# A list schedule with slack before readers on other engines, and with transfers planned at 320 GB/s for 180

## The chip, the cores and the metric

The kernel runs on one core of one Trainium2 chip. The metric is device time in microseconds (us) of one execution; less is better. The core has five engines that work through their own instruction queues in order and wait for each other by semaphores: TensorE (PE, matmuls and transposes; its weight loads are shown as PEld), VectorE (DVE), ScalarE (ACT), GpSimd (POOL) and SyncE (SP, which here issues all transfers). PE writes to PSUM, ACT and DVE read its results there.

## The reference

It is a decoder trunk of two layers on a sequence of 1024 rows of width 1024, in float32.

```python
# layer A: differential attention, 8 heads, each with two pairs (q1,k1), (q2,k2) of width 64
h = rms(x, a_norm)
q, k, v, g = split(h @ a_w_in)                     # 1024 columns each
q, k = rope_partial(rms(q)), rope_partial(rms(k))  # per head and half
a = softmax(mask(q1 @ k1.T / 8)) - lam * softmax(mask(q2 @ k2.T / 8))
o = rms(a @ v, subln) * (1 - lambda_init)
x = x + (o * silu(g)) @ a_w_out
# shared keys and values, then layer B: stick-breaking attention, 16 heads of width 64
k, v = split(rms(x, kv_norm) @ w_kv)
q, g = split(rms(x, b_norm) @ b_w_in)
z = q @ k.T / 8
log_1mb = where(mask, log_sigmoid(-z), 0)
suffix = cumsum_from_the_right(log_1mb) - log_1mb
a = where(mask, exp(log_sigmoid(z) + suffix), 0)
out = x + ((a @ v) * silu(g)) @ b_w_out
```

## The kernel before, in words

Every float32 product is made of three reduced-precision ones: both operands are split into a high and a low part (ACT copies the high part, DVE subtracts), and PE multiplies high by high, high by low and low by high. So a step of a projection is a triple of matmuls into one `proj` accumulator, of 256 or 512 columns. Weights come from DRAM as 256 KB loads into one of three `raw` buffers and are split into `w` tiles (`split_w`); layer A also splits the weights of layer B in advance and writes them back to DRAM (`park`: a `raw` load, a split with `ph` as the high part, two stores).

The work is a sequence of heads. For a head, `qkv_a` or `qkv_b` makes q, k and v by projection; in layer A, q and k are normalised and rotated in a tile `qk` (ACT, DVE, then four instructions on POOL) and transposed by PE (`tr<-ident,qk`). `unit_s` computes scores (`sc`, 64-row matmuls) of blocks of 128 rows and works them into a row of weights `zl` (A: minimum, exponential, sum, normalisation; B: exponential, logarithm, a scan on DVE called `u4k`, exponential). `unit_t` transposes these rows (`tr<-ident,zl`), splits them into `th` and `tl`, and multiplies by the values (`av`). Gated outputs go to DRAM (`og_a`, `og_b`) and come back for the out-projection (`OutProj`), which adds them to residual rows `xr`; those rows are loaded into buffers that held keys and values (`kh`, `kl`, `v`) in `open_rows`. PSUM has two `proj`, three `tr`, one `av` and one double `sc` buffer.

`run_layer` interleaves two threads in the recording: the attention of one head, and as filler the projections of the next head (for the last head: the out-projection of the first half of the rows). What is recorded is not yet the order. Every call goes into `Order.add`, which notes its engine, what it depends on, its priority (its place in the recording, shifted by `rec.priority`) and two planned costs from `Order.cost`: how long it holds its engine, and the lag until others see its result. `Order.issue` is a list scheduler: it goes through planned time, lets each free engine take the ready instruction with the best priority whose buffer is free, and writes the order in which they were taken. Each engine's queue is then that order. An instruction's end, in the plan, releases its readers on other engines and its buffers; readers on the same engine are released when the engine is free. For transfers the plan has one queue: a transfer starts 1.2 us after its issue or behind the one before, takes its size over a rate, and lands 0.8 us later. The plan decides the order alone; on the chip the semaphores decide when.

All compute instructions are emitted by one line of `issue`, so all rows of the profile carry that line, L374; the change moves it to L377.

Of the kernel before, what the change touches and what calls it, by code (L numbers as in the profile page):

```python
# [32 lines left out]
def f32(ap):  # L33
    return ap.bitcast(F32)

class Root:
# [111 lines left out]
class Order:  # L150
# [86 lines left out]
    def cost(self, eng, method, a, kw):  # L237
        n = int(np.prod(a[0].idx.shape)) if isinstance(a[0], L) and a[0].root.space != "dram" else 1
        src = a[1] if len(a) > 1 else None
        if eng == "pe":  # L240
            mv = a[2] if method == "matmul" else a[1]
            if method == "transpose" or mv.dt == F32:
                return n * 0.109 / 128 * (1 if n <= 128 else 2 if n < 512 else 2), 0.17
            t = {512: 0.228, 384: 0.172, 256: 0.12}[n]
            return (t / 2, 0.17) if a[1].p[1] - a[1].p[0] == 64 else (t, 0.17)
        psum = isinstance(src, L) and src.root.space == "psum"
        if eng == "act":
            by = isinstance(kw.get("scale"), L)
            return (0.18 if by else 0.08) + (0.00078 if psum else 0.00086) * n + (0.19 if "accum_out" in kw else 0), 0.17
        if eng == "dve":  # L250
            if method == "tensor_tensor_scan":
                return 0.06 + 0.0021 * n, 0.15
            if method in ("tensor_scalar", "tensor_copy", "memset") and not psum:
                return 0.12 + 0.00055 * n, 0.15
            if method in ("tensor_reduce", "reduce_sum"):
                n = int(np.prod(src.idx.shape))
            if method == "scalar_tensor_tensor":
                return 0.12 + 0.00103 * n, 0.15
            return 0.065 + 0.00105 * n + (0.05 if method == "tensor_tensor_reduce" else 0), 0.15
        if eng == "pool":  # L260
            if method == "affine_select":
                return 0.74 + 0.0008 * n, 0.06
            return (0.13 + 0.0006 * n if method == "memset" else 0.1 + 0.0028 * n), 0.06
        k = a[0] if isinstance(a[0], L) and a[0].root.space != "dram" else a[1]
        size = (k.p[1] - k.p[0]) * int(np.prod(k.idx.shape)) * 4
        return 0.07, size / 180e3

    def issue(self, prepare):

# [9 lines left out]
        early = sum(map(in_la, self.ops))  # L279
        live, nxt = dict.fromkeys(queue, 0), dict.fromkeys(queue, 0)  # L280
        placed, blocked = set(), {s: [] for s in [*queue, None]}
        ready, free = {e: [] for e in self.ENGINES}, dict.fromkeys(self.ENGINES, 0.0)
# [32 lines left out]
        while len(order) < len(self.ops) or events:  # L315
            issued = False
            for e in self.ENGINES:
                if free[e] > now:
                    continue
                while ready[e]:  # L320
                    _, no = heapq.heappop(ready[e])
                    op = self.ops[no]
                    slot = missing(op)
                    if slot != ():
                        blocked[slot].append(no)
                        continue
                    for r in sorted(op.roots, key=lambda r: r.no):
                        if r.slot and r not in placed:
                            placed.add(r)
                            live[r.slot] += 1  # L330
                            nxt[r.slot] += 1
                            unblock(r.slot)
                    op.at, free[e] = now, now + op.took
                    if e == "sp":
                        dma = max(now + 1.2, dma) + op.lag
                        end = dma + 0.8
                    else:
                        end = free[e] + op.lag
                    order.append(op)
                    heapq.heappush(events, (free[e], 0, no))  # L340
                    heapq.heappush(events, (end, 1, no))
                    issued = True
                    break
            if issued:
                continue
            assert events, "no order"
            now = events[0][0]
            while events and events[0][0] <= now:
                _, ended, no = heapq.heappop(events)
                op = self.ops[no]  # L350
                let(op, not ended)
                if not ended:
                    continue
                if in_la(op):
                    early -= 1
                    if not early:
                        unblock(None)
                for r in op.roots:
                    r.left -= 1
                    if r.slot and not r.left:  # L360
                        live[r.slot] -= 1
                        unblock(r.slot)
        self.span = now
        real = lambda x: x.real() if isinstance(x, L) else x
        with self.tc.manual_schedule():
            for op in order:
# [5 lines left out]
                e = self.real[op.eng]  # L372
# [4 lines left out]
def build(tc, ins, out):  # L377
# [7 lines left out]

    mk = lambda name, bufs, **kw: ctx.enter_context(tc.tile_pool(name=name, bufs=bufs, **kw))
    B = {"proj": 2, "sc": 2, "tr": 3, "av": 1, "th": 3, "g2k": 3, "o": 6, "w": 8, "raw": 3, "ta": 1, "g1k": 2, "hpr": 1, "small": 9, "qk": 2, "hpe": -1, "hpw": -1,
         "al": 6, "bl": 8, "tb": 3, "oa": 0, "la": 0, "lb": 8, "lt": 0, "lead": 1.0, "leada": 0.02, "leadb": 0.02, "leadxa": 0.15, "leadxb": 0.1, "holda": 0, "holdb": 0, "c2": 1, "gca": 0, "gcb": 0, "prea": 2, "preb": 1, "warm": 16, "wp": 2, "hpx": -1, "nx": 1, "nk": 6, "hpo": 0, "ob": 2, "late": 400, "ph": 2}
    ORDERS = ((0, 1, 2, 3), (3, 0, 2, 1), (1, 3, 0, 2), (2, 0, 3, 1), (3, 2, 1, 0), (1, 2, 0, 3), (0, 2, 1, 3), (2, 3, 0, 1),
              (1, 0, 3, 2), (3, 2, 0, 1), (2, 3, 1, 0), (1, 0, 2, 3))  # L390
    cp = mk("const", 1)
# [359 lines left out]
    def gate_mul(hd, h, og):  # L751
        for hf in range(2):
            assert hd.done[hf] == 2 and hd.sg[hf] is not None
            o, hi = hd.o[hf], hd.sg[hf].bitcast(F32R)
            pool.tensor_tensor(o, o, hd.sg[hf], ALU.mult)
            (act.copy if B["gc" + "ab"[layer[1]]] else dve.tensor_copy)(hi, o)
            pool.tensor_tensor(o.bitcast(F32R), o, f32(hi), ALU.subtract)
            sp.dma_start(og[hf, 0, :, h, :], f32(hi))
            sp.dma_start(og[hf, 1, :, h, :], o)
# [93 lines left out]
    def run_layer(hds, qkv, unit_s, unit_t, xT, og, op, hfs, extra=()):  # L853
# [5 lines left out]
        f1 = 1 - f0  # L859
# [60 lines left out]
        for h in range(n - 1):  # L920
            main = []
            for i, m in enumerate(order):
                main += unit_s(h, m)
                main += late
                if i == 0 and h > 0:
# [7 lines left out]
        ma, mb, mc, md = last_order  # L933
        op.open_rows(f0, True)
        ss = unit_s(h, ma)
        main = (late + ss if B["lt"] else ss + late) + [(0.0, lambda: gate_mul(hds[h - 1], h - 1, og)),
                                       (0.0, lambda: op.open(f0, op.nk0, n - 1))]
        main += unit_s(h, mb) + unit_t(h, ma) + unit_t(h, mb)
        merge(main, steps[hold:] + fill(n), B["lead"])
        op.finish_gate(f0)  # L940
        main = unit_s(h, mc) + [(0.0, lambda: op.open(f1, 0, n - 1))] + unit_s(h, md) + unit_t(h, mc) + unit_t(h, md)
        steps = fill(n + 1) + [(0.0, lambda: op.open_rows(f1, False))] + fill(n + 2)
        merge(main, steps, B["lead"])
        op.finish_gate(f1)
# [372 lines left out]
```

## Time and profile before

| | |
|---|---|
| median of 3 runs | 1488.15 us (1487.16 to 1489.11) |
| profiled execution | 1487.93 us, span 1486.1 us |
| PE busy | 1403.6 us (94%) |
| weight loads busy | 1181.0 us (79%) |
| DVE, ACT, POOL busy | 1080.6, 920.8, 299.3 us |
| granted TensorE clock, mean | 0.981 |
| moved by transfers | 185.93 MB, 125 GB/s on average |

Layer A ends and layer B starts at about 640 to 720 us; from 1421 us on only the last out-projection is left. In the views by stretches a row has the stretch, its length, the busy time and the number of instructions of PE, PEld, DVE, ACT and POOL in it, the granted clock of TensorE (1 is 2.4 GHz, and half of it the lower level), the busy share of the transfer engines and GB/s. A row of waits has the engine that stood with what it was to write, the engine and tile that released it, the total time, how often, and the longest. In a timeline, what stands in brackets is the idle time of the engine just before the instruction and what ended it.

### The profile page before, as it was taken

To read this page: it belongs to the slowest core of one execution; us is meant where nothing else is said; L and a number is where in the kernel's file an instruction comes from. 1 tells how busy PE (TensorE), PEld (TensorE's weight loads), DVE (VectorE), ACT (ScalarE), POOL (GpSimd) and SP (SyncE) were. 2 spreads that over 40 slices of the span, in tenths; PEclk is the share of its full clock that TensorE was granted. 3 is DMA by queue.
4 is the path that set the end of the run, shared out by engine and by line. 5 is a ranking of instruction groups with operands and counts; after the bars stand their busy time and mean duration, and the time that the engine had idled before them with its cause. 6 is when DMAs were issued, how large, how long until landed. Compare 5 with 4: busy or idle time off the path is not lost.

```text
span 1486.1 us, 24678 instructions
## 1 busy us (share of the span) xinstructions
PE 1403.6 (94%) x8944; PEld 1181.0 (79%) x8944; DVE 1080.6 (73%) x2145; ACT 920.8 (62%) x1834; POOL 299.3 (20%) x545
## 2 busy tenths in 40 slices
PE   7999999999999999868999999999999999998999
PEld 6887878787878787757988777777777878787899
DVE  6588787888888888764531869687878786979941
ACT  6576666666666665432332868686868686878610
POOL 0112221121222121100000124142423241424100
PEclk8999999999999999978999999999999999999999
DMA  5045544454554456343252212121212121143724
GB/s 199 29 150 164 167 153 158 138 175 148 164 177 161 148 182 208 133 179 126 79 170 97 74 58 86 58 86 57 85 54 75 55 74 58 64 168 138 284 85 143
DMA packets 94603, 185.93 MB, mean 125 GB/s; under 512 B 8721, under 2 KB 43793, under 8 KB 93457
## 3 DMA queue, kind: packets, MB, share of 16 engines
q1 hardware_dynamic: 94480, 184.35, 36.9%
q8 instruction: 71, 1.16, 0.3%
q14 instruction: 52, 0.42, 0.1%
HBM read 119.31 MB, written 65.01 MB: 124 GB/s over the span
## 4 chain that ended last, share of the span: by engine, by line
PE 29%; DVE 19%; ACT 9%; issue 3%; POOL 0%; DMA 0%; SPq 0%; DVEq 0%; ACTq 0%; POOLq 0%
PE proj L374 20%; DVE u4k L374 12%; PE av L374 4%; ACT u4k L374 3%; ACT zl L374 3%; PE tr L374 3%; DVE tl L374 2%; PE sc L374 2%; DVE zl L374 1%; DVE o L374 1%; ACT o L374 1%; DVE kl L374 1%; DVE v L374 1%; DVE g2k L374 1%; DVE small L374 0%
## 5 line engine op out<-in xcount | busy, mean ns | idle before, releaser
L374 PE MATMUL proj<-ah,w 128*128 128x512 f32 x1536 | 542.6, 403 | 0.0
L374 PE MATMUL proj<-w,ah 128*128 128x256 f32 x1984 | 382.0, 292 | 7.1 <-ACT w L374 2.7
L374 PEld LDWEIGHTS proj<-ah,w 128*128 128x128 f32 x1536 | 289.0, 188 | 69.6 <-issue 15.4
L374 PEld LDWEIGHTS proj<-w,ah 128*128 128x128 f32 x1984 | 313.9, 194 | 19.3 <-issue 5.8
L374 PE MATMUL proj<-al,w 128*128 128x512 f32 x768 | 300.2, 391 | 0.0
L374 PE MATMUL proj<-w,al 128*128 128x256 f32 x992 | 283.1, 285 | 0.2 <-DVE al L374 0.2
L374 PEld LDWEIGHTS proj<-w,al 128*128 128x128 f32 x992 | 192.3, 194 | 0.7 <-DVE al L374 0.7
L374 DVE TENSOR_TENSOR_SCAN u4k<-zl,u4k 128x768 f32<-128x768 f32 (+4 forms) x96 | 176.7, 1841 | 3.0
L374 PE MATMUL tr<-ident,zl 128*128 128x128 f32 x992 | 152.1, 284 | 22.7 <-DVE zl L374 19.4
L374 ACT ACTIVATE th<-tr 128x512 fp32r<-128x512 f32 (+1 forms) x240 | 126.4, 551 | 67.5 <-PE tr L374 64.5
L374 DVE TENSOR_TENSOR tl<-tr,th 128x512 fp32r<-128x512 f32 (+1 forms) x240 | 144.1, 628 | 32.7 <-ACT th L374 32.0
L374 PE MATMUL av<-th,v 128*128 128x256 f32 x640 | 155.0, 294 | 10.1 <-DVE o L374 5.9
L374 ACT ACTIVATE u4k<-u4k 128x768 f32<-128x768 f32 (+4 forms) x192 | 159.0, 843 | 7.3 <-DVE u4k L374 4.6
L374 PEld LDWEIGHTS proj<-al,w 128*128 128x128 f32 x768 | 144.9, 189 | 19.9
L374 PE MATMUL sc<-kh,q 64*128 64x512 f32 (+2 forms) x768 | 141.8, 387 | 16.4 <-DVE small L374 9.6
L374 PEld LDWEIGHTS tr<-ident,zl 128*128 128x128 f32 x992 | 119.7, 145 | 45.2 <-issue 21.3
L374 PE MATMUL av<-tl,v 128*128 128x256 f32 x480 | 135.4, 302 | 6.4 <-DVE tl L374 5.4
L374 PEld LDWEIGHTS av<-th,v 128*128 128x128 f32 x640 | 113.3, 193 | 29.6 <-issue 11.6
L374 POOL TENSOR_TENSOR o<-o,o 128x512 f32<-128x512 f32 (+1 forms) x56 | 87.9, 1570 | 186.1 <-DVE o L374 171.4
L374 ACT ACTIVATE zl<-zl,small 128x256 f32<-128x256 f32 (+7 forms) x128 | 98.2, 769 | 43.3 <-DVE small L374 43.3
L374 PEld LDWEIGHTS sc<-kh,q 64*128 64x128 f32 x768 | 70.3, 186 | 61.8 <-issue 19.1
L374 DVE SCALAR_TENSOR_TENSOR u4k<-zl,u4k 128x768 f32<-128x768 f32 (+4 forms) x96 | 94.1, 981 | 31.8 <-ACT u4k L374 31.2
(120 smaller groups left out, 1922.3 us busy)
## 6 DMA issues: line engine op xcount, KB each, us to landing
w<-w_kv SPq DMA_DIRECT2D x32, 512.0 KB, 5.1
w<-w_b SPq DMA_DIRECT2D x32, 512.0 KB, 5.0
w<-w_o SPq DMA_DIRECT2D x24, 512.0 KB, 5.7
raw<-in_w_kv_dram SPq DMA_DIRECT2D x32, 256.0 KB, 2.8
w_kv<-ph SPq DMA_DIRECT2D x32, 256.0 KB, 2.2
w_kv<-raw SPq DMA_DIRECT2D x32, 256.0 KB, 2.4
raw<-in_w_b_dram SPq DMA_DIRECT2D x32, 256.0 KB, 2.8
w_b<-ph SPq DMA_DIRECT2D x32, 256.0 KB, 2.5
```

The source lines that it names most:

```text
L374: getattr(e, method)(*[real(x) for x in a], **{k: real(v) for k, v in kw.items()})
```

## The change

Three numbers of the planner are changed; the recorded program is the same. On the planned end of every compute instruction, as others see it, 0.4 us are added. The planned rate of transfers is 320 GB/s instead of 180. In the last head of each layer the attention's steps are recorded with a priority shifted by `-B["ahead"]`, which is 0.

```diff
+MARGIN = 0.4
...
     def cost(self, eng, method, a, kw):
...
-        return 0.07, size / 180e3
+        return 0.07, size / 320e3
...
     def issue(self, prepare):
...
                         dma = max(now + 1.2, dma) + op.lag
                         end = dma + 0.8
                     else:
-                        end = free[e] + op.lag
+                        end = free[e] + op.lag + MARGIN
                     order.append(op)
                     heapq.heappush(events, (free[e], 0, no))
                     heapq.heappush(events, (end, 1, no))
...
+        ahead = lambda steps: [(c, lambda st=st: early(st)) for c, st in steps]
+
+        def early(st):
+            with rec.priority(-B["ahead"]):
+                st()
+
-        main = (late + ss if B["lt"] else ss + late) + [(0.0, lambda: gate_mul(hds[h - 1], h - 1, og)),
+        main = ahead(ss) + late + [(0.0, lambda: gate_mul(hds[h - 1], h - 1, og)),
                                        (0.0, lambda: op.open(f0, op.nk0, n - 1))]
-        main += unit_s(h, mb) + unit_t(h, ma) + unit_t(h, mb)
+        main += ahead(unit_s(h, mb) + unit_t(h, ma) + unit_t(h, mb))
...
-        main = unit_s(h, mc) + [(0.0, lambda: op.open(f1, 0, n - 1))] + unit_s(h, md) + unit_t(h, mc) + unit_t(h, md)
+        main = ahead(unit_s(h, mc)) + [(0.0, lambda: op.open(f1, 0, n - 1))] + ahead(unit_s(h, md) + unit_t(h, mc) + unit_t(h, md))
```

The first place is on PE at the passage from layer A to layer B, before the change. Names are tile, number in the recording and a running number: `sc_1691` are the last scores of layer A's last head, `tr_1707` transposes of the rows `zl_1677` and `zl_1687` made from its last two score steps.

```order
L374 MATMUL tr_1707_8248<-ident_70,zl_1677_8171 128x128
L374 MATMUL tr_1710_8250<-ident_70,zl_1677_8171 128x128
L374 MATMUL tr_1713_8252<-ident_70,zl_1677_8171 128x128
L374 MATMUL sc_1691_8259<-kh_1431_7191,q0_1489_7414 128x512 x2
L374 MATMUL sc_1691_8259<-kl_1432_7198,q0_1489_7414 128x512 x2
L374 MATMUL sc_1691_8259<-kh_1431_7191,q1_1490_7429 128x512 x2
L374 MATMUL tr_1707_8248<-ident_70,zl_1687_8254 128x128
L374 MATMUL tr_1707_8248<-ident_70,zl_1677_8171 128x128
```

The same place in the changed order, where `proj_1763` and `proj_1775` are groups of the out-projection; the dots stand for 3 and for 63 rows, all of the out-projection.

```order
L377 MATMUL sc_1691_8573<-kh_1431_7216,q0_1489_7458 128x512 x2
L377 MATMUL sc_1691_8573<-kl_1432_7229,q0_1489_7458 128x512 x2
L377 MATMUL sc_1691_8573<-kh_1431_7216,q1_1490_7478 128x512 x2
L377 MATMUL proj_1763_8536<-w_1727_8276,ah_1547_7519 128x256
L377 MATMUL proj_1763_8536<-w_1728_8290,ah_1547_7519 128x256
L377 MATMUL proj_1763_8536<-w_1727_8276,al_1548_7521 128x256
...
L377 MATMUL proj_1775_8591<-w_1628_8039,ah_1672_8044 128x256
L377 MATMUL proj_1775_8591<-w_1629_8056,ah_1672_8044 128x256
L377 MATMUL proj_1775_8591<-w_1628_8039,al_1673_8066 128x256
...
L377 MATMUL tr_1707_8552<-ident_70,zl_1687_8557 128x128
L377 MATMUL tr_1707_8552<-ident_70,zl_1677_8433 128x128
```

Before, the transposes of `zl_1687` follow the scores at once; now 72 projection matmuls, single rows all, stand between them.

The second place is SP at the passage, before the change: `raw<-in_a_w_out` loads weights of the out-projection, `kh_1773` and `kl_1774` are residual rows in buffers of keys, `w2_o` stores parked weights.

```order
L374 DMA kh_1773_8267<-in_x_dram 128x1024
L374 DMA kl_1774_8269<-in_x_dram 128x1024
L374 DMA w2_o_87<-ph_1537_8293 128x512
L374 DMA raw_1550_8308<-in_b_w_out_dram 128x512
L374 DMA w2_o_87<-raw_1536_8085 128x512
L374 DMA raw_1632_8345<-in_a_w_out_dram 128x512
L374 DMA w2_o_87<-ph_1551_8357 128x512
L374 DMA w2_o_87<-raw_1550_8308 128x512
L374 DMA raw_1633_8362<-in_a_w_out_dram 128x512
L374 DMA raw_1634_8372<-in_a_w_out_dram 128x512
L374 DMA raw_1635_8384<-in_a_w_out_dram 128x512
```

And in the changed order, from the same load of `raw_1550` on; the dots stand for 15 rows, 10 of them loads of `raw<-in_a_w_out`.

```order
L377 DMA raw_1550_7896<-in_b_w_out_dram 128x512
L377 DMA raw_1632_7910<-in_a_w_out_dram 128x512
L377 DMA w2_o_87<-raw_1536_7775 128x512
L377 DMA w2_o_87<-ph_1551_7952 128x512
L377 DMA raw_1633_7975<-in_a_w_out_dram 128x512
...
L377 DMA raw_1793_8328<-in_a_w_out_dram 128x512
L377 DMA x1_80<-kh_1562_7583 128x1024
L377 DMA x1_80<-kl_1563_7586 128x1024
L377 DMA x1_80<-qk_1564_7214 128x1024
L377 DMA kh_1773_8587<-in_x_dram 128x1024
L377 DMA kl_1774_8589<-in_x_dram 128x1024
```

The loads of `raw_1632` to `raw_1793` stood behind that of `kh_1773` and stand ahead of it now.

The third place is PE in layer A before the change: the transposes of `qk_967` (those at 401.42 us in the trace) with the score step ahead of them.

```order
L374 MATMUL sc_1024_5100<-kh_797_4169,q0_804_4158 128x512 x2
L374 MATMUL sc_1024_5100<-kl_798_4190,q0_804_4158 128x512 x2
L374 MATMUL sc_1024_5100<-kh_797_4169,q1_805_4177 128x512 x2
L374 MATMUL proj_1031_5071<-w_873_4420,ah_4_371 128x256
L374 MATMUL proj_1031_5071<-w_874_4432,ah_4_371 128x256
L374 MATMUL proj_1031_5071<-w_873_4420,al_5_380 128x256
L374 MATMUL tr_1005_5119<-ident_70,qk_967_4815 128x128 x4
L374 MATMUL tr_1008_5127<-ident_70,qk_967_4815 128x128 x4
```

And now, where `proj_1041` is the next group of rows after `proj_1031`; the dots stand for 6 rows of the two projection groups.

```order
L377 MATMUL sc_1024_5125<-kh_797_4214,q0_804_4203 128x512 x2
L377 MATMUL sc_1024_5125<-kl_798_4229,q0_804_4203 128x512 x2
L377 MATMUL sc_1024_5125<-kh_797_4214,q1_805_4219 128x512 x2
L377 MATMUL proj_1031_5086<-w_873_4327,ah_4_364 128x256
L377 MATMUL proj_1031_5086<-w_874_4338,ah_4_364 128x256
L377 MATMUL proj_1031_5086<-w_873_4327,al_5_380 128x256
...
L377 MATMUL proj_1041_5149<-w_871_4286,ah_4_364 128x256
L377 MATMUL proj_1041_5149<-w_872_4304,ah_4_364 128x256
L377 MATMUL proj_1041_5149<-w_871_4286,al_5_380 128x256
L377 MATMUL tr_1005_5160<-ident_70,qk_967_4807 128x128 x4
L377 MATMUL tr_1008_5172<-ident_70,qk_967_4807 128x128 x4
```

From the last matmul of `proj_995`, which completes `qk_967`, to these transposes the old order has 39 projection matmuls and two score steps, the new one 54 and the same two steps.

## Rows read from the trace of the kernel before

**Rows 1.** The page: busy time of each engine, and PE in 40 equal slices.
```profile
PE 1403.6 (94%) x8944; PEld 1181.0 (79%) x8944; DVE 1080.6 (73%) x2145; ACT 920.8 (62%) x1834; POOL 299.3 (20%) x545
...
PE   7999999999999999868999999999999999998999
```

**Rows 2.** Busy time of layer A and of layer B between their ends.
```profile
100.00:600.00 500.00, 475.78 (x3188) 403.36 (x3185) 409.26 (x1038) 326.10 (x745) 102.22 (x144) 1.00 0.52 167
720.00:1300.00 580.00, 568.33 (x3270) 455.07 (x3268) 414.17 (x553) 394.28 (x679) 147.79 (x294) 1.00 0.23 76
```

**Rows 3.** Busy time around the passage from layer A to layer B.
```profile
640.00:650.00 10.00, 5.79 (x30) 4.39 (x31) 7.04 (x20) 3.61 (x7) 0.00 (x0) 0.66 0.93 354
650.00:660.00 10.00, 5.18 (x28) 3.02 (x27) 5.97 (x20) 4.47 (x9) 0.00 (x0) 0.80 0.15 51
660.00:670.00 10.00, 6.27 (x31) 6.27 (x32) 5.32 (x9) 3.89 (x9) 0.41 (x2) 0.52 0.43 152
670.00:680.00 10.00, 4.66 (x22) 3.57 (x20) 3.49 (x6) 2.90 (x6) 0.00 (x0) 0.82 0.35 113
680.00:690.00 10.00, 9.76 (x56) 9.47 (x57) 4.91 (x9) 3.46 (x7) 0.00 (x0) 0.67 0.43 132
```

**Rows 4.** Chain of waits from 640 to 692 us: start, length, what.
```profile
655.89 1.61 PE sc L374 x6
...
663.73 2.18 PE tr L374 x9
...
676.48 2.91 DMA raw<-in_a_w_out_dram
```

**Rows 5.** Timeline of SP from 590 to 700 us: start, length, transfer.
```profile
641.75 0.32 SPq L374 DMA_DIRECT2D w_o<-raw  x1
657.51 0.33 SPq L374 DMA_DIRECT2D kh<-in_x_dram  x1
...
665.81 0.33 SPq L374 DMA_DIRECT2D w_o<-ph  x1
...
667.16 0.42 SPq L374 DMA_DIRECT2D raw<-in_a_w_out_dram  x1
...
676.48 20.08 SPq L374 DMA_DIRECT2D raw<-in_a_w_out_dram  x12
```

**Rows 6.** Busy time of the last 146 us.
```profile
1340.00:1360.00 20.00, 14.75 (x105) 11.48 (x104) 18.96 (x22) 17.81 (x29) 8.31 (x13) 0.89 0.29 111
1360.00:1380.00 20.00, 19.50 (x148) 18.32 (x148) 18.73 (x28) 14.56 (x27) 8.30 (x21) 0.94 0.41 133
1380.00:1400.00 20.00, 16.66 (x123) 14.81 (x123) 18.67 (x25) 17.57 (x28) 6.71 (x6) 0.91 0.96 377
1400.00:1421.00 21.00, 21.00 (x142) 19.68 (x143) 17.47 (x27) 10.18 (x18) 1.12 (x6) 0.92 0.30 118
1421.00:1486.00 65.00, 61.94 (x512) 61.41 (x510) 14.26 (x33) 0.38 (x1) 0.00 (x0) 1.00 0.36 130
```

**Rows 7.** What PE waited for from 100 to 600 us: total, times, longest.
```profile
PE tr L374 <- POOL qk L374: 11.9, 14, 1.9
PE sc L374 <- DVE small L374: 8.0, 9, 1.4
```

**Rows 8.** Timeline in layer A: start, length, instruction, idle time before it.
```profile
401.42 1.09 PE L374 MATMUL tr<-ident,qk 128*128 128x128 f32 x8 [0.54 <-POOL qk L374]
...
402.71 0.40 PE L374 MATMUL proj<-w,ah 128*128 128x256 f32 x2
...
403.07 0.40 PE L374 MATMUL proj<-w,ah 128*128 128x256 f32 x2
```

**Rows 9.** Transfers by line: KB each, median us from issue to landing.
```profile
raw<-in_a_w_out_dram SPq DMA_DIRECT2D x26, 256.0 KB, 2.8
```

**Rows 10.** Waits of ACT on transfers, whole span: total, times, longest.
```profile
ACT w L374 <- DMA raw<-in_a_w_out_dram: 12.1, 6, 5.4
```

**Rows 11.** Busy time of the stretch in which transfers are densest.
```profile
590.00:600.00 10.00, 9.12 (x48) 7.29 (x48) 6.08 (x9) 5.12 (x11) 1.70 (x1) 1.00 1.00 408
```

More of the change, by code (lines that the diff above doesn't have):

```diff
@@ L387, in build @@
     B = {"proj": 2, "sc": 2, "tr": 3, "av": 1, "th": 3, "g2k": 3, "o": 6, "w": 8, "raw": 3, "ta": 1, "g1k": 2, "hpr": 1, "small": 9, "qk": 2, "hpe": -1, "hpw": -1,
-         "al": 6, "bl": 8, "tb": 3, "oa": 0, "la": 0, "lb": 8, "lt": 0, "lead": 1.0, "leada": 0.02, "leadb": 0.02, "leadxa": 0.15, "leadxb": 0.1, "holda": 0, "holdb": 0, "c2": 1, "gca": 0, "gcb": 0, "prea": 2, "preb": 1, "warm": 16, "wp": 2, "hpx": -1, "nx": 1, "nk": 6, "hpo": 0, "ob": 2, "late": 400, "ph": 2}
+         "al": 6, "bl": 8, "tb": 3, "oa": 0, "la": 0, "lb": 8, "lt": 0, "lead": 1.0, "leada": 0.02, "leadb": 0.02, "leadxa": 0.15, "leadxb": 0.1, "holda": 0, "holdb": 0, "c2": 1, "gca": 0, "gcb": 0, "prea": 2, "preb": 1, "warm": 16, "wp": 2, "hpx": -1, "nx": 1, "nk": 6, "hpo": 0, "ob": 2, "late": 400, "ahead": 0, "ph": 2}
     ORDERS = ((0, 1, 2, 3), (3, 0, 2, 1), (1, 3, 0, 2), (2, 0, 3, 1), (3, 2, 1, 0), (1, 2, 0, 3), (0, 2, 1, 3), (2, 3, 0, 1),
```

## The prediction

> **What bounds the kernel now.** I read the page first: PE is busy 1403.6 of 1486.1 us and no other engine is near it; its row of forty slices shows two dents, one at the 17th and 18th slice and one at the 37th [rows 1]. So the time is PE's work plus the time in which PE stands, and an order can only change the second. The view by stretches gives where PE stands. Layer A between its ends (100 to 600 us) has PE idle 500 - 475.8 = 24.2 us, or 4.8%; layer B (720 to 1300 us) 580 - 568.3 = 11.7 us, or 2.0% [rows 2]. The passage between the layers is far worse: 40 us from 640 on hold 21.9 us of PE work, and the clock falls with it, to 0.52 in one slice [rows 3]. The last head of layer B does the same on a smaller scale from 1340 us, with DVE at 18.7 to 19.0 of every 20 us [rows 6].
>
> Why it stands is read from the waits. At the passage the chain of waits goes from the last scores (655.89 us) through the row minimum, the exponentials and the normalisation on DVE and ACT to the transposes at 663.73, and further on through a load of the out-projection's weights, issued at 676.48 [rows 4]. There is nothing else for PE to do in that time. The reason stands in the queue of SP: a load of residual rows into a kh buffer waits from 642 to 657.51, until the last scores have read that buffer. The loads of in_a_w_out are queued behind it: one is issued at 667.16, and then twelve in a run from 676.48 [rows 5]. So work that could have filled PE during the last head's softmax gets its weights only when that softmax is over. In the body of layer A the longest entry is PE waiting for POOL, the transposes of qk after the rotary step, 11.9 us in 14 waits; the scores that wait for DVE come next with 8.0 us [rows 7].
>
> **The change part by part.** Nothing is computed that was not computed before. The three edits act through the planned order alone. The new list entry "ahead" is a shift of priority by zero: nothing. The second, 320e3 for 180e3, lets a 256 KB load take 0.82 us of the planned queue for 1.46 us, so that a lone one lands at 1.2 + 0.82 + 0.8 = 2.82 us after its issue for 3.46 us. The median of the 26 loads of the out-projection weights is 2.8 us [rows 9], and the densest stretch moves 408 GB/s [rows 11], so the new figure is the truer one: the old plan believed its queue full where the chip's was not. The third, 0.4 us on everything that a compute engine gives to another, moves readers back behind other work on their engine; it costs no instruction.
>
> *The passage.* PE stood 4.21 + 4.82 + 3.73 + 5.34 = 18.1 us from 640 to 680, and 0.2 us in the next slice. At half clock it spent 2 x (1 - clock) x 10 us in each slice, that is 6.8, 4.0, 9.6, 3.6 and 6.6 us; by the share in which PE was busy, 20.2 us of work ran at half speed, and half of that, 10.1 us, comes back if PE does not stop [rows 3]. Together 28.4 us. In the new order the last scores are followed by 72 projection matmuls before the transposes that read them. Such matmuls start 0.12 us apart (three from 402.71 to 403.07) [rows 8], so 72 are 8.6 us, and the scores' end to the transposes is 663.73 - 657.50 = 6.2 us [rows 4]: covered, with 2.4 us to spare. Their weights are there because SP now issues the loads of raw_1632 to raw_1793 ahead of the load into kh_1773 and is not held by it. I keep back 4.8% of some 70 us, 3.4 us, for waits of the kind that layer A has: a gain of 25 us, bounded by 0 (the softmax chain ends no earlier and other waits take its place) and 28.4. What is late next, if the loads land late, is ACT's splitting of the weights.
>
> *The body of layer A.* Between the projection group that the rotary chain starts from and the transposes of qk, the place at 401.42 us had 39 projection matmuls and two score steps on PE; in the new order it has 54 and the same two steps: 15 more of 0.12 us are 1.8 us, and the wait there was 0.54 us [rows 8]. All 14 such waits are 0.85 us on average, none over 1.9 us [rows 7]. I take for layer A the idle share that layer B has with the same engines and nearly the same load on ACT and DVE: 2.0% of 500 is 10.1 us, so 14.1 us are gained; ends 0 and 24.2 us. DVE is busy 409 of these 500 us, ACT 326 [rows 2], so they can follow a PE that is 3% quicker. The cover that hides the added distance is the projection work of the next head; where that ran out, a deeper order would wait just as long, only later.
>
> *The body of layer B.* It stands 11.7 us in all [rows 2]; I take a third, 4 us, ends 0 and 11.7.
>
> *The end.* From 1340 to 1400 us PE stands 5.25 + 0.50 + 3.34 = 9.1 us; at the clocks 0.89, 0.94, 0.91 and 0.92 some 11.9 us of its work up to 1421 ran at half speed, which is 6.0 us [rows 6]: 15.1 us together. The new order leaves 390 instead of 504 projection matmuls of 256 columns behind the last one of the attention, so 114 x 0.12 = 13.7 us of them now stand between the steps of the last head. DVE however was busy 56.4 of the 60 us, so a part of the standing is DVE's own length. I take half, 7.5 us; ends 0 and 15.1. From 1421 on PE is busy 61.9 of 65 us and nothing is to be had.
>
> *Sum.* None of the four is safe from being below nothing, since what a margin moves back may simply end later; the price for that is worked out with the third rival and held in the range's upper end. 25 + 14.1 + 4 + 7.5 = 50.6 us. The profiled execution took 1487.93 us, 1.8 us more than its span and 0.2 us less than the median of the runs, 1488.15, so no correction is needed: 1487.9 - 50.6 = 1437 us.
>
> **The rivals.** *More than I take:* all four stretches lose nearly all their standing, 28.4 + 24.2 + 11.7 + 15.1 = 79.4 us. Down to 1408; at seven eighths 1418. For it speaks that nearly every short distance on PE grows in the new order, against it that ACT and DVE are in order too and each has its own bad moments.
>
> *Only the ends are repaired:* the gaps in the layers' bodies stand for buffers, not for order: one accumulator each for scores and for attention times values, two for projections. PE then waits for the previous reader of the buffer wherever the reader is put, and the terms of 14.1 and 4 are nothing: 1487.9 - 25 - 7.5 = 1455 us. Against it: the longest entry names a result (qk from POOL) and not a buffer [rows 7]; for it: the second (scores that wait for DVE) is just such a release, 8.0 of the 24.2 us. The Trainium skill (Perfetto Trace Analysis, under Optimization Strategy) speaks against the change in the same way: a gap that repeats on the engine that should be full can mean that there is too little SBUF or PSUM for the next tile. By that rule layer A's gaps stay; the rows agree with it for a third of the idle time at most.
>
> *Slower:* the transfers are planned too fast. In layer A's queue of ACT, which is in order, 120 splits of loaded weights stand between the exponentials (8 for each of seven heads, and 64 that are parked for layer B); if each stood 0.64 us (1.46 - 0.82) before its load has landed, ACT would wait 76.8 us, and what it passes to PE comes on top. From two thirds on (50.6 of 76.8) the change loses; at four fifths it is 1487.9 + 61.4 - 50.6 = 1499 us. Against it: the measured 2.8 us are what the new plan assumes [rows 9], and ACT's largest wait for transfers so far is 12.1 us in all, of which the blocked queue is the source [rows 10, 5].
>
> *No change:* the readers move back, the waits move with them, 1488 us. The 72 matmuls speak against it.
>
> **How the numbers follow.** The forecast 1437 has 0.57 (its own range 1425 to 1448), more than that 0.13, only the ends 0.18, no change 0.05, slower 0.07. The first three are faster: 0.88. Within 0.2% (3 us, about what a measurement of this kernel can tell from no change): 0.05. The range 1413 to 1468 leaves out no change, slower, the deepest end of the first rival and a passage repaired by half, 0.18 together.
>
> **What would show it.** In the changed kernel's profile the two dents in PE's slices should be gone, the passage should have clock 1.0 with less than 5 us idle, SP should have no stop of 15 us before a load into kh with weights queued behind it, and PE's entry for POOL's qk should fall below 4 us. I am wrong in the passage if the clock still falls there, in layer A if its idle time stays near 24 us under other names, and altogether if ACT waits for raw loads much longer than 12 us.

## The result

The changed kernel takes 1395.19 us (median of 4 runs, 1394.6 to 1396.29) against 1487.66 us (1484.24 to 1489.11): a ratio of 0.9382, 95% interval 0.9365 to 0.94. The forecast of 1437 us and its range, 1413 to 1468, are both missed, on the good side: 92 us were gained where 50.6 were worked out.

The page of the kernel after: its span, busy times, PE in 40 slices, the granted clock in the same slices (tenths), and the shares of the chain that ended last.

```profile
span 1394.5 us, 24717 instructions
...
PE 1365.6 (98%) x8944; PEld 1167.2 (84%) x8944; DVE 1085.4 (78%) x2145; ACT 918.1 (66%) x1834; POOL 289.1 (21%) x545
...
PE   7999999999999999999999999999999999999999
...
PEclk9999999999999999999999999999999999999999
...
PE 79%; DVE 14%; ACT 2%; issue 2%; DMA 1%; POOL 1%; SPq 0%; DVEq 0%; POOLq 0%; ACTq 0%
```

Both dents of [rows 1] are gone. The span fell by 1486.1 - 1394.5 = 91.6 us. PE's idle time fell from 82.5 to 28.9 us, which is 53.6 of them. The other 38.0 us came out of PE's *busy* time, though it runs the same 8944 matmuls. The mean granted clock rose from 0.981 to 0.997. A stretch at a granted clock of 0.981 loses 0.019 of its work, if PE is always at work in it, so the clock explains 0.019 x 1486 - 0.003 x 1394 = 24 us at most. At least 14 us are left. PE changes between kinds of matmul (scores, transposes and so on) 1106 times for 1147, which, at the extra distance of each such change before, is an estimated 3 us. Pauses too short to show fit the remainder, though no view shows them one by one. A matmul's record is longer than its turn, as the timeline after shows (start, length, instruction):

```profile
1273.73 0.28 PE L377 MATMUL proj<-w,al 128*128 128x256 f32 x1
1273.85 0.40 PE L377 MATMUL proj<-w,ah 128*128 128x256 f32 x2
...
1274.09 0.28 PE L377 MATMUL proj<-w,al 128*128 128x256 f32 x1
```

Each such matmul starts 0.12 us after the one before and has a record of 0.28 us, so PE could stand 0.16 us after it and still be called busy.

To see all the loss I counted it in another way, used for every kernel below: each matmul is given the usual distance at which back-to-back ones of its shape start (0.228 us for 512 columns, 0.12 for 256, 0.109 for a 128-column transpose; a pair of 64-row score matmuls counts once), and the trace's own time is read between equal sums of this work. What it takes beyond the sum is lost time, seen as idle or not. The bare work is some 1281 us; the 5.5 us behind the last matmul are left out.

| lost time (us) at work of | before | after | gained | forecast |
|---|---|---|---|---|
| start, 0 to 30 us | 16.4 | 15.0 | 1.4 | 0 |
| layer A's body, 30 to 515 | 64.4 | 34.9 | 29.5 | 14.1 |
| passage, 515 to 640 | 43.3 | 7.3 | 36.0 | 25 |
| layer B's body, 640 to 1140 | 53.1 | 37.8 | 15.3 | 4 |
| end, 1140 to 1281 | 22.4 | 12.8 | 9.6 | 7.5 |

Windows after, for the two bodies, slices of the passage and the end (columns as in [rows 2]):

```profile
100.00:560.00 460.00, 457.01 (x3109) 390.38 (x3107) 398.03 (x1016) 321.07 (x733) 97.05 (x141) 1.00 0.54 171
660.00:1220.00 560.00, 553.39 (x3232) 451.87 (x3233) 427.25 (x552) 394.54 (x685) 146.65 (x294) 1.00 0.24 78
610.00:620.00 10.00, 9.28 (x50) 6.55 (x49) 9.43 (x27) 4.97 (x10) 0.00 (x0) 1.00 0.51 159
640.00:650.00 10.00, 10.00 (x82) 9.46 (x82) 5.49 (x17) 4.97 (x11) 0.00 (x0) 1.00 0.45 159
650.00:660.00 10.00, 10.00 (x87) 10.00 (x86) 9.11 (x30) 6.43 (x16) 0.35 (x2) 1.00 0.17 54
660.00:670.00 10.00, 8.53 (x69) 8.05 (x69) 7.31 (x15) 4.38 (x9) 0.00 (x0) 1.00 0.16 52
1280.00:1300.00 20.00, 16.32 (x127) 13.73 (x126) 19.23 (x29) 16.37 (x31) 8.53 (x24) 1.00 0.87 304
1320.00:1394.00 74.00, 69.34 (x573) 68.35 (x571) 28.42 (x53) 10.22 (x18) 1.05 (x6) 1.00 0.31 114
```

Layer A is idle 2.99 of 460 us, 0.65%, against 4.8% [rows 2]. The passage's work now lies from 565 to 698 us. From 560 to 700 us PE is idle 2.2 us, 0.72 and 1.47 of them in the slices at 610 and 660, and the granted clock is 1.00 in every slice; before, the lowest clock of a slice was 0.52 and the most idle time 5.34 us [rows 3]. What is left stands at the end (16.32 of 20 us), with DVE at 19.23.

PE's waits from 100 to 560 us after, all there are (columns as in [rows 7]):

```profile
PE tr L377 <- POOL qk L377: 1.3, 4, 0.4
PE av L377 <- DVE tl L377: 0.6, 2, 0.3
PE sc L377 <- DVE small L377: 0.5, 1, 0.5
```

The wait for POOL fell from 11.9 us in 14 to 1.3 in 4 [rows 7]. Over the whole span no wait of PE sums to more than 6.0 us. SP after, around the passage (as [rows 5]):

```profile
540.62 3.57 SPq L377 DMA_DIRECT2D raw<-in_a_w_out_dram  x2
...
561.00 0.33 SPq L377 DMA_DIRECT2D kh<-in_x_dram  x1
...
570.09 0.33 SPq L377 DMA_DIRECT2D raw<-in_a_w_out_dram  x1
...
596.93 23.12 SPq L377 DMA_DIRECT2D raw<-in_a_w_out_dram  x10
```

The run of ten loads of the out-projection's weights at 596.93 us now comes before the last scores of layer A, and the transposes of their rows follow these without a wait of PE, 8.7 us later; the rows between are all projection matmuls:

```profile
640.84 0.40 PE L377 MATMUL sc<-kh,q 64*128 64x512 f32 x2
...
649.91 1.15 PE L377 MATMUL tr<-ident,zl 128*128 128x128 f32 x9
```

Two numbers of the planner did this; the experiments ask which did what, and why.

### The profile page after: what moved, and what is told of

Its sections match the earlier page's. It is cut to its first block, busy times and chain, and to the rows that moved or that the text cites. A ratio compares the mean times of both kernels' runs of the same rounds, so it can differ in the third digit from the quotient of the medians.

```text
span 1394.5 us, 24717 instructions
## 1 busy us (share of the span) xinstructions
PE 1365.6 (98%) x8944; PEld 1167.2 (84%) x8944; DVE 1085.4 (78%) x2145; ACT 918.1 (66%) x1834; POOL 289.1 (21%) x545
## 4 chain that ended last, share of the span: by engine, by line
PE 79%; DVE 14%; ACT 2%; issue 2%; DMA 1%; POOL 1%; SPq 0%; DVEq 0%; POOLq 0%; ACTq 0%
PE proj L377 53%; PE tr L377 9%; PE av L377 9%; DVE u4k L377 7%; PE sc L377 7%; DVE tl L377 1%; DVE zl L377 1%; DVE o L377 1%; DVE small L377 1%; ACT zl L377 1%; ACT u4k L377 1%; DVE w L377 1%; DVE v L377 0%; DVE kl L377 0%; DVE raw L377 0%
## 5 line engine op out<-in xcount | busy, mean ns | idle before, releaser
L377 PE MATMUL proj<-w,ah 128*128 128x256 f32 x1984 | 376.3, 289 | 4.1 <-DVE v L377 2.0
L377 PEld LDWEIGHTS proj<-ah,w 128*128 128x128 f32 x1536 | 289.0, 188 | 68.6 <-issue 13.4
L377 PEld LDWEIGHTS proj<-w,ah 128*128 128x128 f32 x1984 | 309.0, 192 | 14.4 <-issue 4.9
L377 DVE TENSOR_TENSOR_SCAN u4k<-zl,u4k 128x768 f32<-128x768 f32 (+4 forms) x96 | 181.5, 1890 | 3.0
L377 PE MATMUL tr<-ident,zl 128*128 128x128 f32 x992 | 147.8, 276 | 7.4 <-DVE zl L377 2.9
L377 PE MATMUL av<-th,v 128*128 128x256 f32 x640 | 148.1, 288 | 0.9 <-DVE o L377 0.8
L377 PE MATMUL av<-tl,v 128*128 128x256 f32 x480 | 129.8, 291 | 6.1 <-DVE tl L377 6.0
L377 PEld LDWEIGHTS tr<-ident,zl 128*128 128x128 f32 x992 | 116.6, 142 | 20.6 <-issue 10.0
L377 PEld LDWEIGHTS av<-th,v 128*128 128x128 f32 x640 | 110.6, 189 | 14.5 <-issue 3.1
```

The lines of the kernel that those rows point to most:

```text
L377: getattr(e, method)(*[real(x) for x in a], **{k: real(v) for k, v in kw.items()})
```

## The experiments

A ratio is always to the kernel before on the same chip, with its 95% interval. The lost time of each, by the stages of the table above:

| kernel | median us | ratio | start | A | passage | B | end |
|---|---|---|---|---|---|---|---|
| before | 1487.66 | 1 | 16.4 | 64.4 | 43.3 | 53.1 | 22.4 |
| after | 1395.19 | 0.9382 | 15.0 | 34.9 | 7.3 | 37.8 | 12.8 |
| slack alone | 1441.12 | 0.9701 | 14.7 | 35.4 | 49.5 | 38.1 | 16.4 |
| rate alone | 1449.56 | 0.976 | 15.5 | 66.5 | 14.7 | 52.3 | 11.9 |
| rate, dearer small operations | 1431.91 | 0.9638 | 13.9 | 55.6 | 10.1 | 51.4 | 11.9 |
| before, kh loads moved | 1485.5 | 0.9986 | 16.0 | 65.9 | 41.8 | 53.1 | 20.8 |
| slack, no planned queue | 1401.02 | 0.9408 | 17.1 | 30.7 | 12.3 | 39.0 | 13.4 |
| rate, slack on readers only | 1394.81 | 0.937 | 13.8 | 32.7 | 13.2 | 37.8 | 8.9 |
| rate, slack on buffers only | 1446.93 | 0.9731 | 14.5 | 64.6 | 13.1 | 51.7 | 12.9 |
| rate, slack before PE only | 1433.86 | 0.9635 | 15.0 | 58.3 | 11.5 | 49.3 | 10.2 |
| rate, slack 0.2 | 1396.74 | 0.9384 | 14.3 | 41.6 | 7.0 | 35.9 | 9.5 |
| rate, slack 0.8 | 1405.61 | 0.9448 | 18.2 | 27.5 | 22.8 | 30.3 | 15.6 |
| readers 0.8, dearer small operations | 1406.21 | 0.945 | 15.8 | 27.3 | 25.4 | 31.4 | 15.5 |
| 0.8 in bodies, 0.2 in last heads | 1398.93 | 0.9406 | 13.7 | 29.1 | 20.9 | 30.1 | 12.7 |

**Each part alone.** First the slack without the rate:

```diff
-        return 0.07, size / 320e3
+        return 0.07, size / 180e3
```

> The changed kernel with the old transfer rate (180 GB/s) in the plan, the 0.4 us of slack kept. Theory S (the slack does the layers' bodies, the rate opens the passage): PE's matmul work of the bodies loses about 30 us in layer A and 15 us in layer B as in the changed kernel, but the passage keeps some 20 to 30 us of its standing: 1415 to 1425 us. Rival P (the slack alone does it all): 1395 to 1400 us. Rival R (the rate does most of it): 1450 us or more.

Measured 1441.12 us, ratio 0.9701 (0.9683 to 0.9718). Then the rate without the slack:

```diff
-MARGIN = 0.4
+MARGIN = 0.0
```

> The changed kernel with the slack set to 0, the planned rate of 320 GB/s kept. Theory S: the passage opens (25 to 36 us), the bodies stand as before: 1452 to 1463 us. Rival P: no change, 1484 to 1490 us. Rival R: 1440 us or less.

Measured 1449.56 us, ratio 0.976 (0.9739 to 0.9781). The first is above its forecast, since the passage got worse, not just no better; the second is a little below. The table parts them cleanly: the slack makes both bodies (35.4 and 38.1, as in the changed kernel) and nothing of the passage; the rate makes most of the passage and nothing of the bodies. The end each repairs alone, the slack 6.0 us of it and the rate 10.5. Windows of the passage with the slack alone:

```profile
600.00:610.00 10.00, 4.60 (x19) 3.53 (x20) 6.38 (x18) 4.65 (x9) 0.00 (x0) 0.50 0.53 160
610.00:620.00 10.00, 6.52 (x45) 4.76 (x44) 6.99 (x21) 4.77 (x10) 0.00 (x0) 1.00 0.97 388
620.00:630.00 10.00, 6.53 (x41) 6.54 (x42) 4.90 (x8) 3.35 (x6) 0.35 (x2) 0.66 0.23 82
```

and with the rate alone, the only slice there with less than 8.8 us of PE:

```profile
640.00:650.00 10.00, 8.66 (x58) 8.05 (x60) 8.14 (x27) 4.97 (x11) 0.00 (x0) 0.83 0.41 114
```

With the slack alone PE is busy 4.60 us in the first slice, at a granted clock of 0.50, the lower level; with the rate alone the worst slice has 8.66 us and 0.83. With the rate alone PE's wait for POOL's qk from 100 to 580 us is as long as in [rows 7], while that of the scores has shrunk:

```profile
PE tr L377 <- POOL qk L377: 14.4, 14, 2.6
PE sc L377 <- DVE small L377: 2.7, 5, 0.6
```

The two ratios multiply to 0.9468; together they give 0.9382, 13 us more. By the table that is the passage: the slack alone makes it 6.2 us worse, the rate alone 28.6 better, and both 36.0 better, 13.6 more than the sum. Without the rate the slack only adds to the late weights; with it, it takes the passage from 14.7 to 7.3. Against that, 6.9 us of the end are counted by both.

**Is it wrong costs that the slack covers?** The plan has a difference of single columns hold DVE 0.066 us, and a function of 1 to 16 columns hold ACT 0.08 to 0.09 us. The trace of before, grouped by form (mean ns behind the comma):

```profile
L374 DVE TENSOR_TENSOR small<-small,lam 128x1 f32<-128x1 f32 x64 | 15.7, 245 | 2.2
...
L374 DVE TENSOR_TENSOR small<-small,small 128x1 f32<-128x1 f32 x48 | 7.6, 159 | 6.4 <-ACT small L374 4.8
...
L374 ACT ACTIVATE small<-small,eps 128x16 f32<-128x16 f32 x16 | 4.9, 306 | 14.2 <-DVE small L374 14.1
...
L374 ACT ACTIVATE small<-small 128x1 f32<-128x1 f32 x16 | 3.2, 203 | 0.5
```

A record compares with the plan's hold and lag together, since the lag counts until others see the result: 0.22 us on DVE and 0.25 to 0.26 on ACT. By that the plan is short by at most some 0.1 us. A reader on the same engine is planned behind the hold alone, and there it is clearly short: behind a reciprocal of two columns, planned at 0.067 us, DVE's next instruction starts 0.199 us later (median of 64). Larger operations are planned well: `tl` of 512 columns holds DVE 0.603 us in the plan and 0.600 in the trace, `th` holds ACT 0.479 in both. Nor is the lag too short: it is 0.15 us for DVE and 0.17 for ACT and PE, while a waiting ACT or DVE starts 0.03 to 0.04 us behind the end of the record that released it (medians). So I took the rate, no slack, and a floor on the planned time:

```diff
-MARGIN = 0.4
+MARGIN = 0.0
...
+        took = max(took, {"dve": 0.17, "act": 0.25}.get(eng, 0.0))
```

> The planned rate of 320 GB/s, no slack, but no DVE instruction is planned shorter than 0.17 us and no ACT instruction shorter than 0.25 us (the plan has 0.07 to 0.13 and 0.08 to 0.09 for the smallest, the trace 0.15 to 0.17 and 0.25). Theory C (the slack works because the plan's small costs are too low, so correct costs would do as well): within 10 us of the changed kernel, 1395 to 1405 us. Theory V (the slack works because it takes up what no plan knows, queues that drift): within 10 us of the kernel with the rate alone, 1445 to 1460 us.

Measured 1431.91 us, ratio 0.9638 (0.9619 to 0.9656), outside both bands. The floor wins 11 of layer A's 31.6 us (66.5 to 55.6; to 34.9 with the slack) and 1 of layer B's 14.5. So small operations planned too short are not layer B's loss. For layer A the 11 us are not all truer costs for certain: a reader on another engine is now planned 0.32 or 0.42 us behind, later than the records have it, and that is slack too. POOL's costs were left as they were. An operation on qk of 256 columns is planned at 0.82 us and 0.06 till others see it, and the records take 0.89 to 0.90, with 0.055 us more until a waiting PE starts; whether the rest of layer A's gain covers errors of that kind, or waits that no fixed cost can foresee, was not tested.

**Slack for results or for buffers?** An instruction's planned end releases its readers on other engines and its buffers; the change delays both. Each alone, with the new rate:

```diff
                     heapq.heappush(events, (free[e], 0, no))
+                    early_end = end if e == "sp" else end - MARGIN
                     heapq.heappush(events, (end, 1, no))
+                    heapq.heappush(events, (early_end, 2, no))
...
-                let(op, not ended)
-                if not ended:
+                if ended < 2:
+                    let(op, not ended)
                     continue
```

So readers go at event 1, with the slack, and buffers at event 2, without it. For buffers only, events 1 and 2 change places.

> The changed kernel with the 0.4 us on readers on other engines alone; a buffer is planned free without it. Theory D (the slack works on results): 1393 to 1402 us. Rival U (it works on the buffers, above all the single accumulators): 1425 to 1450 us, near the kernel with the rate alone.

> The changed kernel with the 0.4 us on the planned release of buffers alone; readers are released without it. Theory D: 1440 to 1452 us, near the rate alone. Rival U: 1393 to 1410 us.

Measured: readers only 1394.81 us, 0.937 (0.9352 to 0.9388), the whole gain; buffers only 1446.93 us, 0.9731 (0.9706 to 0.9755), no better than the rate alone (0.9739 to 0.9781) within the intervals. Layer A's gaps did not stand for buffers. That is also the answer to the Trainium skill (Perfetto Trace Analysis, Optimization Strategy), by which repeated gaps can mean too little SBUF or PSUM: here no buffer was added and the gaps closed.

**Is it enough to move PE's instructions back?** Slack only where the reader is on PE:

```diff
-        def let(op, same):
+        def let(op, same, on_pe):
...
-                if (u.eng == op.eng != "sp") == same:
+                if (u.eng == op.eng != "sp") == same and on_pe in (None, u.eng == "pe"):
```

with readers on PE released at the late end, all others and the buffers at the early one.

> The changed kernel with the 0.4 us only where the reader is an instruction of PE; readers on ACT, DVE and POOL and the buffers have none. Theory E (only the last hop to PE counts, since PE is the engine whose standing costs): 1393 to 1403 us. Rival H (the slack must add up along the chain over ACT, DVE and POOL, as in the chain of 13 instructions ahead of the transposes of qk): 1412 to 1440 us, with PE's waits for qk from POOL back above 6 us.

Measured 1433.86 us, 0.9635 (0.9616 to 0.9653). PE still waits, from 100 to 580 us:

```profile
PE tr L379 <- POOL qk L379: 8.8, 8, 1.7
PE sc L379 <- DVE small L379: 7.0, 5, 1.5
PE av L379 <- ACT th L379: 3.2, 5, 0.8
```

Layer A keeps 58.3 us lost. The slack at PE's own door is worth 8 us there (66.5 to 58.3), the slack at the other hops, among ACT, DVE and POOL and to the stores, the other 26 (to 32.7): one 0.4 does not carry a chain that goes ACT, DVE, POOL, PE, and one at each of its hops does. Slack at the other hops alone was not run, so what it would give without PE's is open.

**How much slack?**

```diff
-MARGIN = 0.4
+MARGIN = 0.2
```

> The changed kernel with 0.2 us of slack instead of 0.4. If the slack takes up errors of the plan of a few tenths of a microsecond per hop, half of it gives more than half of the bodies' 45 to 55 us (rate alone 1449.6, changed kernel 1395.2): 1400 to 1418 us. If it matters only once it is larger than some wait, little: 1430 to 1448 us.

and 0.8 in the same place:

> The changed kernel with 0.8 us of slack. If 0.4 us already covers nearly all waits of the bodies (they stand 3 to 4 us per 500 us in layer A), 0.8 gives at most 6 us more and may lose at the ends, where there is no other work to put between: 1388 to 1403 us. If the deeper order runs out of buffers: 1410 us or more.

Measured 1396.74 us, 0.9384 (0.9368 to 0.9401), for 0.2, and 1405.61 us, 0.9448 (0.9427 to 0.9469), for 0.8. Half is as good as the whole, and a little better than its band. The double is better in both bodies (27.5 and 30.3), and worse at the passage and the end by 18.3 us; its time lies between what the two theories expected. Two trials to keep the first without the second. With 0.8 for readers only and the floor on small operations:

> A version meant to beat the changed kernel: 0.8 us on readers alone (buffers planned free without it), and the small instructions of DVE and ACT planned at 0.17 and 0.25 us. What is left to gain in the bodies is some 10 us, in the passage and at the end some 10: 1383 to 1395 us if the slack can grow where the buffers are not charged for it; 1395 to 1405 us if the deeper order costs at the ends what it gains.

Measured 1406.21 us, 0.945 (0.9428 to 0.9472), just above its bands: the same picture. And 0.8 in the heads of the bodies, 0.2 in the start and in each layer's last head:

```diff
-MARGIN = 0.4
+MARGIN = 0.2
+DEEP = 0.8
...
-                        end = free[e] + op.lag + MARGIN
+                        end = free[e] + op.lag + op.margin
...
+        rec.margin = DEEP        # before the heads 0 to n - 2 are recorded
...
+        rec.margin = MARGIN      # before the last head
```

> A version meant to beat both: 0.8 us of slack on what is recorded while all heads but the last of a layer are worked on, 0.2 us on the start and on the last head of each layer with its out-projection. By PE's matmul work, 0.8 us stood 15 us less than 0.4 in the bodies of the two layers and 16 us more in the passage, and 0.2 us stood about as little as 0.4 in the passage and 3 us less at the end. If these add up: 1378 to 1386 us. If the passage is spoiled by what the deeper bodies leave undone before it: 1393 to 1405 us.

Measured 1398.93 us, 0.9406 (0.938 to 0.9432): no gain over the changed kernel. Layer A's body is as with 0.8 (29.1), and the passage stays bad (20.9) though its own head has 0.2 only, with which it loses 7.0 behind bodies of 0.2: it is the deep body that spoils it. The slice where PE stands most:

```profile
560.00:570.00 10.00, 5.70 (x35) 4.51 (x34) 9.90 (x22) 3.20 (x6) 5.79 (x8) 0.83 0.64 209
```

DVE is full there (9.90 of 10 us) while PE has 5.70 us of work. In the next two slices PE has 6.64 and 7.49 us with DVE at 7.97 and 5.00, so a full DVE is not the whole of it. Which instructions the deep order pushed there was not settled, and no run tells it. None of these versions beats the changed kernel; slack on readers only and slack 0.2 equal it within what can be told.

**Was the kh load what held the weights up?** The prediction's cause of the passage. In the finished order of the kernel *before*, the two loads of residual rows are moved behind the last load of weights:

```diff
+        moved = [op for op in order if op.eng == "sp" and op.no in (4715, 4716)]   # kh_1773, kl_1774
+        order = [op for op in order if op not in moved]
+        at = [op.no for op in order].index(4794) + 1                               # raw_1793
+        order[at:at] = moved
```

> The kernel before, with one edit of its finished order: SP's two loads of residual rows into kh_1773 and kl_1774 stand behind the loads of raw_1632 to raw_1793 instead of ahead of them. Theory K (the prediction's: the kh load that waits for the last scores holds up the weights of the out-projection): the weights come up to 15 us earlier and the time falls by 5 to 15 us, to 1473 to 1483 us. Theory Q (the weights are late because the plan put their loads and everything around them late; the kh load is only one of several that wait there): within 3 us of the kernel before.

Measured 1485.5 us, 0.9986 (0.9973 to 0.9998): next to nothing, and 1.5 us of the passage's 43.3. SP in that kernel:

```profile
642.90 0.32 SPq L378 DMA_DIRECT2D w_o<-raw  x1
666.35 0.32 SPq L378 DMA_DIRECT2D w_o<-ph  x1
...
667.73 0.38 SPq L378 DMA_DIRECT2D raw<-in_a_w_out_dram  x1
...
676.45 19.68 SPq L378 DMA_DIRECT2D raw<-in_a_w_out_dram  x12
```

The stop of 15 us before the kh load is gone, and the weights come when they came before, at 667 and 676 us: SP now waits at the next entry of its queue, the store of a parked weight. In an in-order queue the entry that waits is not the cause if the one behind it would wait as long.

**Then why are they ordered so late?** The planned transfer queue is one after another: each starts behind the one before. In layer A the chip moves 167 to 171 GB/s on average (the last column of [rows 2] and of the windows after). A queue planned at 180 GB/s is nearly full on average, and the bursts beyond that would pile up in it. Planned landings would slip, and with them all that hangs on them: splits, parks, the next loads. To test this, the slack with the *old* rate, but each transfer for itself:

```diff
-        return 0.07, size / 320e3
+        return 0.07, size / 180e3
...
-                        dma = max(now + 1.2, dma) + op.lag
+                        dma = now + 1.2 + op.lag
```

> The changed kernel with the old rate of 180 GB/s, but without the plan's transfer queue: each transfer is planned to land 1.2 us + its size over the rate + 0.8 us after its own issue, whatever is ahead of it. A lone 256 KB load is thus planned as late as before (3.46 us). Theory Q (the old rate hurt because the planned queue fell behind): the passage opens as in the changed kernel, 1392 to 1402 us. Rival L (it hurt because each load was planned to land 0.64 us late): like the kernel with the slack alone, 1435 to 1445 us.

Measured 1401.02 us, 0.9408 (0.9386 to 0.9429): with each load still planned at the old 3.46 us the passage opens (12.3 us lost, against 49.5 with the queue). SP of this kernel:

```profile
534.43 6.59 SPq L377 DMA_DIRECT2D raw<-in_a_w_out_dram  x4
...
595.68 25.93 SPq L377 DMA_DIRECT2D raw<-in_a_w_out_dram  x10
```

and of the one with the slack and the queue at 180 GB/s:

```profile
607.94 4.21 SPq L377 DMA_DIRECT2D raw<-in_a_w_out_dram  x2
...
624.04 14.75 SPq L377 DMA_DIRECT2D raw<-in_a_w_out_dram  x4
...
656.74 18.53 SPq L377 DMA_DIRECT2D raw<-in_a_w_out_dram  x11
```

The same run of loads goes out some 60 us earlier (595.68 against 656.74) once the planned backlog is gone, at unchanged times for a single load. So it was the backlog, not the time of a load.

## Why the prediction was wrong, point by point

- *That an order can only change PE's standing, read as idle time.* The first sentence of the working held, but its measure did not: the terms for the bodies were sums of idle time, and a part of what an order can win lies inside busy time. Layer B, at a granted clock of 1.00 both times, shows it. Per matmul, before is 580 / 3270 = 177.4 ns and after 560 / 3232 = 173.3; idle fell from 3.57 to 2.05 ns, 5.0 us over 3270 matmuls, and busy from 173.8 to 171.2 ns, 8.4 us. The 4 us forecast sized the visible part rightly (5.0) and could not contain the rest, at any bound: its end of 11.7 was below the 15.3 us gained.
- *Layer A, 14.1 us.* The mechanism was right: POOL's qk was the longest wait and is nearly gone, by order and not by buffers. The size failed at one step, "I take for layer A the idle share that layer B has", 2.0%. It went to 0.65%; layer B was no floor, it had the same illness (its own share went from 2.0% to 6.61 / 560 = 1.2%). By the count per matmul, 500 / 3188 = 156.8 ns became 460 / 3109 = 148.0: of 28 us, 21 were idle and 7 busy. The place at 401.42 us was judged by its own distance on PE, 15 more matmuls. After the change that very wait still measures 0.42 us (0.54 before); the other ten went because the ACT, DVE and POOL queues in front of it were ordered with slack too, as the run with slack before PE only shows.
- *The passage, 25 us.* That 72 out-projection matmuls would cover the softmax came true (640.84 to 649.91 us, no wait). The bound of 28.4 us was drawn around 640 to 690 us, and the lost time lay in the work from 598 to 766 us, 43.3 us in all; 7.3 stayed, where 3.4 were kept back. The dent of [rows 1] already shows it: it takes three slices, the 17th to the 19th, 594 to 706 us, not two. The named cause, the kh load that held the weights on SP, was wrong: moving it gave next to nothing, and with the slack, opening the planned queue at the old load time gave most of the passage. [rows 5] had a sign of this: behind the kh load SP stands again until 665.81, at the store of a parked weight.
- *The end, 7.5 us.* 9.6 came. The term was near, but which of the two numbers did it is open, since the slack alone does 6.0 and the rate alone 10.5. What still stands there goes with DVE, as was argued.
- *The rivals.* "Only the ends are repaired" fell with the runs for readers and for buffers; the end it would give, 1455 us, is near what the rate alone gives (1449.56), for another reason. "Transfers planned too fast" fell: ACT's waits on these loads are 15.3 us in 5 after against 12.1 in 6 [rows 10], and PE does not see them. "More than I take" had the right side, but its full 79.4 us were no ceiling, since they were the same idle time and half clock in the same four stretches.

So the direction, the places and the passage's mechanism on PE stood; what failed was a ceiling taken for the loss from what the views call idle, a floor taken from a stage with the same fault, and a cause read from the waiting queue entry. Of the 41 us that the sum fell short, 15 are layer A's, 11 each layer B's and the passage's, 2 the end's and 1 the start's.

## What to carry to other kernels

When engines run in order and a list schedule sets the order, plan each hop to another engine a little longer than it is (0.2 us did here): a reader that was planned late cost little here while there was other work, and one placed too early stopped its whole engine at the hop. Too much is possible: 0.8 us spoiled the passage. Let the planned transfer queue have clearly more rate than the real average traffic, or its backlog pushes loads back far from where the profile shows any full queue. And size what an engine can win by the bare time of its instructions, not by its idle time, and try the entry behind a blocked one before naming the blocked one as the cause.

## What the runs showed that was not expected

- Of the 91.6 us of span, 38.0 came out of PE's busy time; half clock explains at most 24 of them. With records of 0.28 us and starts 0.12 us apart, a pause under some 0.16 us behind a 256-column matmul would leave no idle time in the trace.
- Single-column differences on DVE have records of 0.16 to 0.25 us and functions of 1 to 16 columns on ACT 0.20 to 0.31 us, two to four times what this planner lets them hold their engine, while the holds of `tl` and `th` with 512 columns fit to 0.003 us.
- The clock loss was not a matter of its own. Before, 0.52 stood behind two slices with PE busy 5.79 and 5.18 of 10 us [rows 3], and with the slack alone 0.50 in a slice with 4.60; where the standing went, the granted clock stayed at 1.00 through the passage, with nothing done for the clock.
